# Fetching the residual by pairs of column blocks, and a fourth group of seven products in the down stages' second pair

## The chip, the cores and the metric

The kernel runs on one core of one Trainium2 chip. The metric is the time of one execution on the device, in microseconds (us); lower is better. Before the change it is 1809.0 us, the median of three runs.

## The reference

One layer over 256 rows x of width 2048, all in float32:

```python
x = x + 0.5 * swiglu(rms_norm(x, ffn1_norm), ffn1_w_gate, ffn1_w_up, ffn1_w_down)
h = rms_norm(x, mix_norm);  [u | q | k | v] = h @ w_in
x = x + concat(rms_norm(GLU(S5(u))), rms_norm(stick_breaking(q, k, v))) @ w_out
x = x + 0.5 * swiglu(rms_norm(x, ffn2_norm), ffn2_w_gate, ffn2_w_up, ffn2_w_down)
x = x + rms_norm((p @ w_ple_proj) * sigmoid(rms_norm(x, ple_norm) @ w_ple_gate), ple_post_norm)

def swiglu(h, w_gate, w_up, w_down):
    return (silu(h @ w_gate) * (h @ w_up)) @ w_down      # inner width 5632
```

The change lies in the two products with `w_down`: 256 x 5632 by 5632 x 2048, once in each half FFN.

## The kernel before

**Precision.** A float32 product is made of three matmuls of a rounded type: high by high, low by high and high by low. `split` (L179 to 191) makes both halves of an operand: the high half is an ACT cast (L182), the low half a DVE subtraction (L185) that needs it. A weight is split when it has come in. Its 128x(4x512) float32 tile of 1 MB, called `raw`, comes by one transfer on SP's queue (L369 for a column, L585 for a chunk), into a pool of five raw buffers. Each half of a tile, 128x1024, is one split; its two results go into a ring of seven weight pairs (`weight_pair`, L342: four named `whi`/`wlo`, three `shi`/`slo`). DVE thus cannot be more than seven pairs ahead of TensorE (PE).

**The down stage** (in `ffn`, from L826 to `pools.close()`) has the 5632 inner positions in 11 blocks `kb` of 512, the 2048 output columns in four blocks of 512, taken as two pairs, and the rows in two tiles `t` of 128. For one pair and one inner block there are two ways:

- a *column* (`column`, L688): each of the two column blocks (side 0, side 1) by itself, 24 matmuls a side in `gemm_half` (L386 high weights, L379 low weights). A side takes one raw tile and two splits. The activation block is split once (`act`, giving `hhi`, `hlo`) and kept for the next use; two such are kept at a time.
- a *chunk* (`chunk`, L663): both sides at once, by seven products in place of eight, 42 matmuls (L567, L570, L572) in place of 48. Its two raw tiles give the quarters b11, b21, b12, b22. DVE makes three sums of them (`add`, L578), POOL issues a transfer that adds b22 to b12 in place (L671), and seven splits follow, products 1, 5, 6, 4, 2, 3, 7 in this order. A chunk also needs the activations in summed form (`sum_forms`: four 128x256 row sums on DVE, L524, and a split into `nhi`, `nlo`).

After a pair's last chunk, `opened` (L839) adds the seven products' sums into the residual x: one ACT copy, two DVE additions from PSUM (L843, L848) and six gathers of 128x512 (`gather`, L837). The remaining columns then finish one side after the other; at each side's end (`end`) two gathers and two transposes (`nxt.block`, L220) start that block's way to the next stage.

**The order** is written out by hand in `plans`, one row per pair: ("c", kb) a column on both sides, ("s", kb) a chunk, ("f", kb) a summed form ahead of its chunk, ("a", ...) the columns that end one side after the other, side 1 in the reversed order. Chunks of pair 2 are 2, 1 and 0; columns 10, 9, 3, 4 and then 5, 6, 7, 8. A scheduler orders the instructions of each engine from this.

**The residual** x is fetched at the start of each down stage (`fetch_x`, L826): eight POOL transfers of 128x512 (L151) into two raw tiles, one for each row tile, from the input in the first FFN and from `scr_x` in the second. They are held until the stage's end, so that three raw buffers are left for weights.

**SP's queue** also carries the finished blocks to the next stage: `turn_quarters` (L233) issues 16 small transfers `h<-mid` for each column block, among the weight loads.

The stages are seen in the trace at about 446 to 704 us (first FFN) and 1445 to 1701 us (second).

Of the kernel before, what the change touches and what calls it, by code (L numbers as in the profile page):

```python
# [9 lines left out]
F32 = mybir.dt.float32  # L10
# [6 lines left out]
P = 128  # L17
# [9 lines left out]
NB = 512  # L27
# [6 lines left out]
def layer_kernel(ctx: ExitStack, tc: tile.TileContext, a: dict, shapes: dict, out: bass.AP):  # L34
# [9 lines left out]
    TT = T // P  # L44
    ND = D // NB
# [8 lines left out]
    wp = ctx.enter_context(tc.tile_pool(name="wts", bufs=4))  # L54
# [8 lines left out]
    def uid(s):  # L63
        count[0] += 1
        return f"{s}_{count[0]}"
# [16 lines left out]
    def small(n=8):  # L82
        return smp.tile([P, 8], F32, tag="sm", name=uid("sm"))[:, :n]
# [24 lines left out]
    def put_off(steps, fn, *args):  # L108


        def g():
            for _ in range(steps):
                yield
            fn(*args)

        return start(g())
# [22 lines left out]

    xt = [[], []]  # L140

    def place_x():
        for t in range(TT):
            x = wp.tile([P, ND, NB], F32, tag="raw", name=uid("x"), bufs=5)
            xt[t][:] = [x[:, n, :] for n in range(ND)]

    def fetch_x(rows):
        place_x()
        for n in range(ND):
            for t in range(TT):  # L150
                nc.gpsimd.dma_start(xt[t][n], rows[t * P : (t + 1) * P, n * NB : (n + 1) * NB])  # L151

    scr_x = dramp.tile([T, D], F32, name="scr_x")
# [361 lines left out]
    def sum_forms(pool, u, kind="n"):  # L515

        sums = pool.tile([P, 2, NB], F32, tag="sum", name=uid("rows"), bufs=2)
        s = sums.rearrange("p j n -> p (j n)").rearrange("p (z j x b) -> p z j x b", z=4, j=2, b=32)
        (a11, a21), (a12, a22) = ([u[:, k : k + 2, 4 * t : 4 * t + 4] for t in range(TT)] for k in (0, 2))
        for z, (x, y, op) in enumerate((  # L520
            (a21, a22, ALU.subtract), (s[:, 0], a11, ALU.subtract),
            (a11, a21, ALU.subtract), (a12, s[:, 1], ALU.add),
        )):
            nc.vector.tensor_tensor(out=s[:, z], in0=x, in1=y, op=op)  # L524
        both = halves(kind)
        split(*both, sums.rearrange("p j n -> p (j n)").rearrange("p (z t) -> p z t", z=4))
        return both
# [175 lines left out]
    def ffn(i, xn, nxt, bg=None):  # L703
# [7 lines left out]
        side = ExitStack()  # L711
# [18 lines left out]
        for f in range(NF):  # L730
# [9 lines left out]
            if f >= early or f in alone:  # L740
# [17 lines left out]
                s = Seven(xn, lambda kb: sums[kb], ((wg, f * NB), (wu, f * NB)), sevens, turns)  # L758
# [64 lines left out]
                )  # L823
            put_off(2, turned, hp, f, hh)

        fetch_x(a["x"][0] if bg else scr_x)  # L826

        def rows(k):
            return hT[k // 2][:, k % 2 * 4 : k % 2 * 4 + 4]
# [6 lines left out]
        def gather(x, ps, scale):  # L836
            nc.vector.scalar_tensor_tensor(out=x, in0=ps, scalar=scale, in1=x, op0=ALU.mult, op1=ALU.add)  # L837

        def opened(s, n):  # L839
# [5 lines left out]
            for t in range(TT):  # L845
# [9 lines left out]
                ("c", 10),  # L855
            ),
            (
                ("c", 10), ("c", 9), ("s", 2), ("c", 3), ("s", 1), ("f", 0), ("c", 4), ("s", 0), ("a", (5, 6, 7, 8)),
            ),
        )  # L860
        parts, forms = {}, {}
# [13 lines left out]
        for n in range(0, ND, 2):  # L875

            def end(side):
                m = n + side
                for t, z in enumerate(((2, 4), (3, 8))[side]):
                    gather(xt[t][m], s.bank(z), 0.5)  # L880
                put_off(0 if m == ND - 2 or m == ND - 1 and m < nxt.early else 2, nxt.block, m)

            s = Seven(kept, summed, ((wd, n * NB), (wd, (n + 1) * NB)), sevens, turns)
            plan = plans[n // 2]
            left = sum(kind == "s" for kind, _ in plan)
            for kind, kb in plan:
                final = (kind, kb) == plan[-1]
                if kind == "f":
                    forms[kb] = sum_forms(sevens, rows(kb))
                    continue  # L890
                if kind == "s":
                    left -= 1
                    s.chunk(kb, () if left else shared)
                    if not left:
                        put_off(0, opened, s, n)
                    continue
                for side in range(2):
                    s.column(side, (kb,) if kind == "c" else kb[:: 1 - 2 * side], final)
                    if final:
                        end(side)  # L900
        pools.close()
# [737 lines left out]

    n1, nm, n2, npl = Normed("ffn1_norm", load_turned), Normed("mix_norm"), Normed("ffn2_norm", kinds="hhnn", late=0), Normed("ple_norm", late=0)  # L1640
    ffn(1, n1, nm, s5_prep)

    w_in = a["w_in"]
# [75 lines left out]
    mix.close()  # L1719

    ffn(2, n2, npl)


# [62 lines left out]
    with sums_phase("sums3") as sevens:  # L1786
        forms = {1: sum_forms(sevens, whole_rows(sevens, npl(1)), "h")}
        s = Seven(npl, forms.get, ((wg, 0), (wg, NB)), sevens, sevens)
# [16 lines left out]
    n = ND - 1  # L1805
# [11 lines left out]
    t = 0  # L1817
    sigmoid(gate, t, next(gates))
    ple(n, t, gate, next(projs))
    s = small(1)  # L1820
# [7 lines left out]
    t = 1  # L1828
# [152 lines left out]
```

## Time and profile before

| | |
|---|---|
| time, median of 3 runs | 1809.0 us (1808.81 to 1809.14) |
| the profiled execution's own time | 1810.11 us |
| its span | 1808.3 us |
| PE busy, 8892 matmuls | 1801.0 us |
| DVE busy | 1614.2 us |
| ACT busy | 1081.4 us |
| first down stage, 446 to 704 us: PE / DVE busy | 257.18 / 236.02 us |
| second down stage, 1445 to 1701 us: PE / DVE busy | 256.00 / 235.54 us |

The profile follows one execution. A row of the timeline gives start, duration, engine, line, operation, output and inputs; a bracket at its end tells how long the engine was idle before it, and what ended that. `xN` joins N such instructions in a row.

### The profile page before, as it was taken

How to read it: one execution, taken by the hardware profiler on the slowest of the kernel's cores; microseconds unless marked ns; L12 is line 12 of the kernel's file. 1: busy time of each engine (PE TensorE's matmuls, PEld its weight loads, DVE VectorE, ACT ScalarE, POOL GpSimd, SP SyncE). 2: the span in 40 equal slices, each digit the busy share in tenths (PEclk: the TensorE clock that was granted, in tenths of full speed). 3: DMA queues.
4: the chain of work that ended last, by engine and by line, in shares of the span. 5: the costliest groups of instructions: out<-in, count | busy, mean ns of one | idle time of the engine just before them, and what ended most of it. 6: DMA issues, size and time to landing. Idle time of an engine off the chain costs nothing.

```text
span 1808.3 us, 24274 instructions
## 1 busy us (share of the span) xinstructions
PE 1801.0 (100%) x8892; PEld 1492.8 (83%) x8892; DVE 1614.2 (89%) x1894; ACT 1081.4 (60%) x1264; POOL 137.1 (8%) x196
## 2 busy tenths in 40 slices
PE   9999999999999999999999999999999999999998
PEld 8888888888888878888898888888888888888887
DVE  7998889999999898887867899999999999989875
ACT  7445456555666566456895566555565566666664
POOL 0020100000000001112121000000000000000000
PEclk9999999999999999999999999999999999999999
DMA  9689967787776667765646777776767787666663
GB/s 377 214 277 315 279 220 234 242 268 220 257 248 228 209 237 229 258 244 179 204 153 209 248 278 239 266 263 222 233 232 248 236 273 244 231 209 221 206 245 128
DMA packets 108662, 430.49 MB, mean 238 GB/s; under 512 B 24608, under 2 KB 48576, under 8 KB 66144
## 3 DMA queue, kind: packets, MB, share of 16 engines
q1 hardware_dynamic: 96096, 390.10, 60.9%
q0 software_dynamic: 12160, 38.55, 10.0%
q8 instruction: 69, 1.13, 0.2%
q14 instruction: 49, 0.40, 0.1%
q10 hardware_dynamic: 288, 0.31, 0.1%
HBM read 372.41 MB, written 10.88 MB: 212 GB/s over the span
## 4 chain that ended last, share of the span: by engine, by line
PE 90%; DVE 4%; DMA 2%; issue 1%; SPq 1%; ACT 1%; DVEq 0%; ACTq 0%; POOL 0%; POOLq 0%
PE acc L386 29%; PE acc L379 15%; PE aux L386 13%; PE aux L379 7%; PE acc L567 5%; PE acc L572 5%; PE acc L570 5%; PE aux L570 3%; PE aux L567 3%; PE aux L572 3%; DMA raw<-in_ffn_w_down 2%; DVE wlo L185 1%; SPq L233 1%; DVE slo L185 1%; DVE sum L578 1%
## 5 line engine op out<-in xcount | busy, mean ns | idle before, releaser
L185 DVE TENSOR_TENSOR wlo<-raw,whi 128x1024 fp32r<-128x1024 f32 x478 | 576.3, 1221 | 96.7 <-ACT whi L182 94.6
L182 ACT CAST whi<-raw 128x1024 fp32r<-128x1024 f32 x478 | 495.2, 1050 | 267.2 <-PE acc L386 139.8
L386 PE MATMUL acc<-whi,nhi 128*128 128x512 f32 x850 | 331.7, 392 | 0.0
L386 PE MATMUL acc<-whi,nlo 128*128 128x512 f32 x850 | 329.7, 389 | 0.0
L379 PE MATMUL acc<-wlo,nhi 128*128 128x512 f32 x850 | 240.5, 389 | 0.1
L185 DVE TENSOR_TENSOR slo<-raw,shi 128x1024 fp32r<-128x1024 f32 x186 | 226.2, 1216 | 8.7 <-ACT shi L182 7.2
L182 ACT CAST shi<-raw 128x1024 fp32r<-128x1024 f32 x186 | 195.1, 1049 | 42.1 <-DMA raw<-in_ffn_w_down 22.5
L182 ACT CAST whi<-sum 128x1024 fp32r<-128x1024 f32 x83 | 87.5, 1054 | 168.8 <-DVE sum L578 159.3
L386 PEld LDWEIGHTS acc<-whi,nhi 128*128 128x128 f32 x850 | 159.7, 188 | 33.7 <-ACT whi L182 0.2
L379 PEld LDWEIGHTS acc<-wlo,nhi 128*128 128x128 f32 x850 | 159.4, 188 | 33.7 <-DVE wlo L185 0.5
L386 PEld LDWEIGHTS acc<-whi,nlo 128*128 128x128 f32 x850 | 159.6, 188 | 32.4
L182 ACT CAST shi<-sum 128x1024 fp32r<-128x1024 f32 x61 | 64.3, 1054 | 105.5 <-DVE sum L578 104.8
L671 POOL DMA_DIRECT2D raw<-raw x47 | 41.4, 880 | 1034.8 <-DVE sum L578 827.9
L578 DVE TENSOR_TENSOR sum<-sum,raw 128x1024 f32<-128x1024 f32 x96 | 117.1, 1220 | 0.9
L185 DVE TENSOR_TENSOR wlo<-sum,whi 128x1024 fp32r<-128x1024 f32 x83 | 101.2, 1221 | 3.1 <-ACT whi L182 2.2
L386 PE MATMUL aux<-whi,nhi 128*128 128x512 f32 x244 | 95.0, 389 | 0.0
L386 PE MATMUL aux<-whi,nlo 128*128 128x512 f32 x244 | 94.9, 389 | 0.0
L185 DVE TENSOR_TENSOR slo<-sum,shi 128x1024 fp32r<-128x1024 f32 x61 | 74.5, 1221 | 0.7
L379 PE MATMUL aux<-wlo,nhi 128*128 128x512 f32 x244 | 75.1, 389 | 0.0
L578 DVE TENSOR_TENSOR sum<-raw,raw 128x1024 f32<-128x1024 f32 x48 | 58.5, 1219 | 5.3 <-DMA raw<-in_ffn_w_down 5.2
L567 PE MATMUL acc<-whi,hhi 128*128 128x512 f32 x154 | 60.2, 391 | 0.0
L570 PE MATMUL acc<-whi,hlo 128*128 128x512 f32 x154 | 59.9, 389 | 0.0
(427 smaller groups left out, 3539.7 us busy)
## 6 DMA issues: line engine op xcount, KB each, us to landing
raw<-in_ffn_w_down SPq DMA_DIRECT2D x88, 1024.0 KB, 4.9
raw<-in_ffn_w_gate SPq DMA_DIRECT2D x87, 1024.0 KB, 7.3
raw<-in_ffn_w_up SPq DMA_DIRECT2D x87, 1024.0 KB, 5.6
raw<-in_w_in SPq DMA_DIRECT2D x32, 1024.0 KB, 5.7
raw<-raw POOLq DMA_DIRECT2D x50, 512.0 KB, 5.7
raw<-in_w_out SPq DMA_DIRECT2D x16, 1024.0 KB, 4.9
raw<-in_w_ple_gate SPq DMA_DIRECT2D x16, 1024.0 KB, 5.3
hT<-mid SPq DMA_DIRECT2D x160, 64.0 KB, 4.7
```

Source lines behind the costliest of these rows:

```text
L182: copy = nc.scalar.copy(hi, src)
L185: rest = nc.vector.tensor_tensor(out=lo, in0=src, in1=hi.bitcast(F32), op=ALU.subtract)
L233: nc.sync.dma_start(out[32 * q : 32 * q + 32].rearrange("p (t i w) -> p t i w", t=TT, i=4)[:, :, i], mid[32 * i : 32 * i + 32, q].rearrang ...
L379: nc.tensor.matmul(ps[t], lhsT=lh, rhs=lo[:, j, cols], start=False, stop=stop and j == 1, skip_group_check=joined,)
L386: nc.tensor.matmul(ps[t], lhsT=(ahi, alo)[i][:, 2 * h + j, t * P : (t + 1) * P], rhs=hi[:, j, cols], start=start and j == 0 and i == 0, st ...
L567: nc.tensor.matmul(ps, lhsT=lh[j], rhs=hi[:, j], start=begin and j == 0, stop=False, skip_group_check=joined)
L570: nc.tensor.matmul(ps, lhsT=ll[j], rhs=hi[:, j], start=False, stop=False, skip_group_check=joined)
L572: nc.tensor.matmul(ps, lhsT=lh[j], rhs=lo[:, j], start=False, stop=z in final and j == 1, skip_group_check=joined)
L578: nc.vector.tensor_tensor(out=t, in0=x, in1=y, op=ALU.add)
L671: nc.gpsimd.dma_start(b12, b22, accum_op=ALU.add)
```

## The change

`place_x` goes; `fetch_x` gets a pair as its argument and fetches only that pair's two column blocks, for both row tiles, into one raw tile. Pair 0 is fetched where all of x was before, so that four raw buffers are left for weights; the second pair's fetch is an entry ("x", 1) of the second plan, after chunk 0, from where three are left. In the second plan block 5 becomes a chunk, with its summed form just ahead; blocks 4 and 6 have their side 0 ahead of it, through a new entry ("o", kb), and their side 1 at the end, and the last entry now gives each side's columns itself.

```diff
-    def place_x():
-        for t in range(TT):
-            x = wp.tile([P, ND, NB], F32, tag="raw", name=uid("x"), bufs=5)
-            xt[t][:] = [x[:, n, :] for n in range(ND)]
-
-    def fetch_x(rows):
-        place_x()
-        for n in range(ND):
+    def fetch_x(rows, pair):
+        x = wp.tile([P, ND, NB], F32, tag="raw", name=uid("x"), bufs=5)
+        for n in range(2 * pair, 2 * pair + 2):
             for t in range(TT):
+                xt[t][n] = x[:, 2 * t + n % 2, :]
                 nc.gpsimd.dma_start(xt[t][n], rows[t * P : (t + 1) * P, n * NB : (n + 1) * NB])
...
-        fetch_x(a["x"][0] if bg else scr_x)
+        fetch_x(a["x"][0] if bg else scr_x, 0)
...
-                ("c", 10), ("c", 9), ("s", 2), ("c", 3), ("s", 1), ("f", 0), ("c", 4), ("s", 0), ("a", (5, 6, 7, 8)),
+                ("c", 10), ("c", 9), ("s", 2), ("c", 3), ("s", 1), ("f", 0), ("o", 4), ("s", 0), ("x", 1), ("o", 6),
+                ("f", 5), ("s", 5), ("a", ((7, 8), (8, 7, 6, 4))),
...
+                if kind == "x":
+                    fetch_x(a["x"][0] if bg else scr_x, kb)
+                    continue
...
-                for side in range(2):
-                    s.column(side, (kb,) if kind == "c" else kb[:: 1 - 2 * side], final)
+                for side in range(1 if kind == "o" else 2):
+                    s.column(side, kb[side] if kind == "a" else (kb,), final)
```

What DVE does in the first FFN's second pair after the split for chunk 0's fourth product (`slo` of a `sum`, the first row of each piece). `raw`, `sum`, `rows` and `hT` are weight tiles, their sums, row sums and activations; before, `raw_1077` and `raw_1085` are the first ending columns:

```order
L185 TENSOR_TENSOR slo_1068_5744<-sum_1066_5741,shi_1067_5743 128x1024
L185 TENSOR_TENSOR slo_1072_5764<-raw_1055_5700,shi_1071_5763 128x1024
L185 TENSOR_TENSOR wlo_1074_5774<-raw_1055_5700,whi_1073_5773 128x1024
L185 TENSOR_TENSOR hlo_1076_5784<-hT2_449_2679,hhi_1075_5783 128x1024
L185 TENSOR_TENSOR wlo_1079_5790<-raw_1077_5787,whi_1078_5789 128x1024
L185 TENSOR_TENSOR slo_1081_5794<-raw_1077_5787,shi_1080_5793 128x1024
L837 SCALAR_TENSOR_TENSOR x_757_4236<-sg_1082_5809,x_757_4236 128x512
L837 SCALAR_TENSOR_TENSOR x_757_4236<-acc_988_5350,x_757_4236 128x512
```

and with the change, where `raw_1072` is block 6 and `raw_1080` and `raw_1081` are chunk 5:

```order
L181 TENSOR_TENSOR slo_1062_5705<-sum_1060_5702,shi_1061_5704 128x1024
L181 TENSOR_TENSOR slo_1066_5725<-raw_1049_5661,shi_1065_5724 128x1024
L181 TENSOR_TENSOR wlo_1068_5735<-raw_1049_5661,whi_1067_5734 128x1024
L181 TENSOR_TENSOR hlo_1071_5750<-hT3_581_3325,hhi_1070_5749 128x1024
L181 TENSOR_TENSOR slo_1074_5756<-raw_1072_5753,shi_1073_5755 128x1024
L181 TENSOR_TENSOR wlo_1076_5760<-raw_1072_5753,whi_1075_5759 128x1024
L520 TENSOR_TENSOR rows_1077_5787<-hT2_449_2679 128x256 x2
L520 TENSOR_TENSOR rows_1077_5787<-rows_1077_5787,hT2_449_2679 128x256
L181 TENSOR_TENSOR hlo_1083_5801<-hT2_449_2679,hhi_1082_5800 128x1024
L520 TENSOR_TENSOR rows_1077_5787<-hT2_449_2679,rows_1077_5787 128x256
L574 TENSOR_TENSOR sum_1084_5804<-raw_1080_5796,raw_1081_5798 128x1024
L181 TENSOR_TENSOR wlo_1086_5808<-raw_1080_5796,whi_1085_5807 128x1024
```

Where the gathers into x began, one side of block 6 and the chunk's sums and splits now stand; the gathers come after chunk 5's last split.

SP's queue around chunk 2's two loads (L585 before, L581 with the change) and the load of column 3 (`raw_1004`, `raw_1003`), with the transfers of the first pair's blocks (`h<-mid`) between them. Before:

```order
L369 DMA raw_973_5286<-in_ffn1_w_down 128x2048
L233 DMA h_956_5191<-mid_955_5190 32x2x128 x4
L585 DMA raw_978_5324<-in_ffn1_w_down 128x2048
L233 DMA h_956_5191<-mid_955_5190 32x2x128 x2
L585 DMA raw_979_5326<-in_ffn1_w_down 128x2048
L233 DMA h_956_5191<-mid_955_5190 32x2x128 x6
L233 DMA h_963_5229<-mid_955_5190 32x2x128 x4
L233 DMA h_956_5191<-mid_955_5190 32x2x128 x4
L233 DMA h_963_5229<-mid_955_5190 32x2x128 x8
L369 DMA raw_1004_5440<-in_ffn1_w_down 128x2048
```

With the change:

```order
L365 DMA raw_972_5281<-in_ffn1_w_down 128x2048
L581 DMA raw_977_5319<-in_ffn1_w_down 128x2048
L229 DMA h_955_5186<-mid_954_5185 32x2x128 x4
L581 DMA raw_978_5321<-in_ffn1_w_down 128x2048
L229 DMA h_955_5186<-mid_954_5185 32x2x128 x8
L229 DMA h_962_5224<-mid_954_5185 32x2x128 x4
L229 DMA h_955_5186<-mid_954_5185 32x2x128 x4
L229 DMA h_962_5224<-mid_954_5185 32x2x128 x8
L365 DMA raw_1003_5435<-in_ffn1_w_down 128x2048
```

Chunk 2's first load has moved ahead of all of these transfers, its second two places up; the load of column 3 still has 28 of them ahead of it.

POOL's queue over the second pair, before:

```order
L671 DMA raw_915_4997<-raw_915_4997 128x1024
L671 DMA raw_979_5326<-raw_979_5326 128x1024
L671 DMA raw_1019_5534<-raw_1019_5534 128x1024
L671 DMA raw_1055_5700<-raw_1055_5700 128x1024
L1269 MEMSET m3_1132_6123 128x2048
```

With the change, where `x_1069` is the second part of x and `raw_1049` belongs to chunk 0:

```order
L667 DMA raw_978_5321<-raw_978_5321 128x1024
L667 DMA raw_1018_5529<-raw_1018_5529 128x1024
L147 DMA x_1069_5744<-in_x 128x512 x4
L667 DMA raw_1049_5661<-raw_1049_5661 128x1024
L667 DMA raw_1081_5798<-raw_1081_5798 128x1024
```

The fetch stands ahead of chunk 0's accumulating transfer, though the plan has it after that chunk, and chunk 5's is new.

## The prediction

> **What bounds the kernel now.** I read the page first. Three of its lines say where to look: the span, the busy times, and the chain of work that ended last.
>
> ```profile
> span 1808.3 us, 24274 instructions
> PE 1801.0 (100%) x8892; PEld 1492.8 (83%) x8892; DVE 1614.2 (89%) x1894; ACT 1081.4 (60%) x1264; POOL 137.1 (8%) x196
> PE 90%; DVE 4%; DMA 2%; issue 1%; SPq 1%; ACT 1%; DVEq 0%; ACTq 0%; POOL 0%; POOLq 0%
> ```
>
> PE is idle for 1808.3 - 1801.0 = 7.3 us of the whole span, so nothing that only lets data come sooner can gain more than that. DVE is second with 89%, but that is an average. The view by windows, over the middle of the second pair of either down stage, shows the local share (columns: window, length, busy time of PE, PEld, DVE, ACT, POOL with instructions, clock, DMA share, GB/s):
>
> ```profile
> 612.00:669.00 57.00, 57.00 (x253) 47.22 (x252) 53.05 (x56) 37.53 (x42) 1.77 (x2) 1.00 0.69 240
> 1611.00:1668.00 57.00, 57.00 (x253) 47.22 (x252) 53.97 (x57) 38.45 (x42) 1.73 (x2) 1.00 0.73 244
> ```
>
> PE has no gap, and DVE lacks 57 - 53.05 = 3.95 us. What DVE waits for in these two windows is short:
>
> ```profile
> DVE wlo L185 <- ACT whi L182: 3.1, 1, 3.1
> DVE sum L578 <- DMA raw<-in_ffn_w_down: 0.4, 1, 0.4
> ```
> ```profile
> DVE slo L185 <- ACT shi L182: 3.3, 1, 3.3
> ```
>
> One wait in each window is nearly all of DVE's idle time. After it, DVE works without a pause while PE does too: two engines at their limit, and DVE is never more than a pair or two ahead. The timelines give both paces. PE (column block 3's first matmul, and the same place 12 matmuls on):
>
> ```profile
> 618.08 0.39 PE L386 MATMUL acc<-whi,hhi 128*128 128x512 f32 x1
> 620.80 0.39 PE L386 MATMUL acc<-whi,hhi 128*128 128x512 f32 x1
> ```
>
> So a matmul takes 2.72 / 12 = 0.2267 us. DVE:
>
> ```profile
> 611.17 1.22 DVE L185 TENSOR_TENSOR hlo<-hT,hhi 128x1024 fp32r<-128x1024 f32 x1
> 615.46 2.36 DVE L185 TENSOR_TENSOR wlo<-raw,whi 128x1024 fp32r<-128x1024 f32 x2 [3.07 <-ACT whi L182]
> ...
> 634.69 0.42 DVE L524 TENSOR_TENSOR rows<-rows,hT 128x256 f32<-128x256 f32 x1
> 635.02 0.42 DVE L524 TENSOR_TENSOR rows<-hT 128x256 f32<-128x256 f32 x1
> ...
> 636.83 1.22 DVE L185 TENSOR_TENSOR slo<-raw,shi 128x1024 fp32r<-128x1024 f32 x1
> 637.97 1.22 DVE L185 TENSOR_TENSOR nlo<-rows,nhi 128x1024 fp32r<-128x1024 f32 x1
> 639.10 1.22 DVE L185 TENSOR_TENSOR wlo<-raw,whi 128x1024 fp32r<-128x1024 f32 x1
> ...
> 652.39 1.23 DVE L185 TENSOR_TENSOR slo<-sum,shi 128x1024 fp32r<-128x1024 f32 x1
> ...
> 659.21 0.69 DVE L837 SCALAR_TENSOR_TENSOR x<-sg,x 128x512 f32<-128x512 f32 x1
> 659.82 1.28 DVE L837 SCALAR_TENSOR_TENSOR x<-acc,x 128x512 f32<-128x512 f32 x2
> ```
>
> The starts are (639.10 - 636.83) / 2 = 1.135 us apart for a 128x1024 operation (a split's second half, or an addition; "wide" below), 0.33 for a row sum, 0.61 for a 128x512 gather. I price by starts, since rows of 1.22 us overlap. [...] By full lengths the total below would be about 4 us higher.
>
> **The change part by part.**
>
> *Seven products for block 5 in place of two columns.* A chunk has 42 matmuls, two columns have 48: -6 in each of the two down stages, -12 x 0.2267 = **-2.72 us** of PE. On DVE a chunk needs 10 wide operations (3 sums, 7 splits) = 11.4 us against 42 x 0.2267 = 9.52 of PE: it eats the lead. A column on both sides has 4 splits and an activation split = 5.7 against 10.88: it builds lead. The change trades the second for the first and adds a summed form (4 row sums and a split, 1.3 + 1.1 us).
>
> [...]
>
> *DVE's lead at chunk 0.* Before, its fourth product needs its second half at:
>
> ```profile
> 654.34 0.62 PE L572 MATMUL acc<-slo,hhi 128*128 128x512 f32 x2
> ```
>
> DVE ends that split at 652.39 + 1.23 = 653.62, a lead of 0.72. Afterwards block 4 has one side before chunk 0, so PE asks 24 x 0.2267 = 5.44 earlier, at 648.90; DVE has two splits less, 2.27, and starts earlier. Why earlier: SP's queue before,
>
> ```profile
> 588.84 0.53 SPq L585 DMA_DIRECT2D raw<-in_ffn_w_down  x1
> ...
> 591.99 0.33 SPq L585 DMA_DIRECT2D raw<-in_ffn_w_down  x1
> 592.37 16.03 SPq L233 DMA_DIRECT2D h<-mid  x22
> 608.50 0.53 SPq L369 DMA_DIRECT2D raw<-in_ffn_w_down  x1
> ```
>
> and ACT, whose wait ends when that last load lands:
>
> ```profile
> 614.38 2.00 ACT L182 CAST whi<-raw 128x1024 fp32r<-128x1024 f32 x2 [3.62 <-DMA raw<-in_ffn_w_down]
> ```
>
> The load of column 3 stands behind 28 activation transfers and, before, behind two chunk loads among them; the second is issued 3.15 us after the first, of which its buffer's release accounts for 3.15 - 0.53 - 2 x 0.73 (16.03 / 22) = 1.2. With four weight buffers one chunk load stands ahead of those transfers and the other finds its buffer free: 1.2 + 0.33 of issue = 1.5 us earlier at least. The load's own 614.38 - 608.50 = 5.9 us may come down towards the 4.9 of the page's row (below), and the transfers run less beside loads: 2.5 and more. DVE's restart moves from 615.46 to no later than 614 and no earlier than 611.17 + 1.14 = 612.3, where the work ahead ends (611.4 if that activation split is put behind). I take 612.4, near that end. Then chunk 0's split ends at 653.62 - 3.06 - 2.27 - 0.37 (the DMA wait above) = 647.9: lead 1.0, no stall.
>
> *From chunk 0's fourth product to chunk 5's.* PE: a chunk and one side of block 6, 9.52 + 5.44 = 14.96 us. DVE, counted in the changed order: 16 wide operations and 4 row sums, 16 x 1.135 + 4 x 0.33 = 19.5. It loses 4.55 against a lead of 1.0: **a stall of 3.55**. From there to column 8: PE 48 matmuls = 10.88, DVE 6 wide and 8 of 128x512 (the opening of the sums into x) = 6.8 + 4.9 = 11.7, 0.8 more. Together **4.3 us per down stage** (3.3 with restart at 611.4, 5.9 at 614). Later columns have one side each (5.44 of PE against 3.4 of DVE), so DVE recovers and no more is lost. In the second stage DVE restarts after an idle time of the same length, and its lead at chunk 0's fourth product is smaller:
>
> ```profile
> 1613.86 1.22 DVE L185 TENSOR_TENSOR slo<-raw,shi 128x1024 fp32r<-128x1024 f32 x1 [3.28 <-ACT shi L182]
> ...
> 1651.49 1.22 DVE L185 TENSOR_TENSOR wlo<-raw,whi 128x1024 fp32r<-128x1024 f32 x1
> ```
> ```profile
> 1653.14 0.62 PE L572 MATMUL acc<-wlo,hhi 128*128 128x512 f32 x2
> ```
>
> (1653.14 - 1651.49 - 1.22 = 0.43). I take 4.3 for it too: **+8.6** in all.
>
> *A stall that goes.* The first stage has one now, at column 6:
>
> ```profile
> 669.97 0.49 PE L386 MATMUL acc<-whi,hhi 128*128 128x512 f32 x1
> 671.23 0.50 PE L386 MATMUL acc<-whi,hlo 128*128 128x512 f32 x1 [0.76 <-DVE hlo L185]
> ```
>
> 1.26 - 0.23 = 1.03 us. DVE got there late for want of a load of this order of the plan; that place is gone: **-1.03**.
>
> *The second fetch of x.* Four transfers on POOL's queue, ahead of chunk 0's accumulating transfer. They need the buffer of chunk 1's second tile, free after its last split, two splits ahead of the row sums at 634.69 above, so by about 632 or sooner; the accumulation waits for chunk 0's first sum, 7 wide operations before the split that ends at 647.9, so until about 640. The fetch before:
>
> ```profile
> L151 POOL DMA_DIRECT2D x<-in_x x8: 546/562/729, 446.7 to 455.8; - x8
> ```
>
> At 0.56 us each they are issued by 635: no delay. Gathers need x near 672. Priced at nothing; without that cover the accumulation would be late by the difference, 0 to 2 us. Four fetches fewer at the stage's start, and one more raw buffer there, can gain at most what PE lacks of the span.
>
> *Handover.* The last sides have four columns as before, but the next stage's first loads stand behind 12 to 16 activation transfers in place of ahead of them, and at the end of the second stage PE waits already:
>
> ```profile
> 1716.90 0.50 PE L567 MATMUL acc<-shi,nhi 128*128 128x512 f32 x1 [0.59 <-ACT shi L182]
> ```
>
> From this row I bound the extra wait between 0 and 3 us for both stages (up to five times this row, once or twice), **+1.0**, nearer the bottom, since DVE has 4 x 3.4 = 13.6 us of work for 21.8 us of PE there.
>
> *Sum:* -2.72 - 1.03 + 8.6 + 1.0 = **+5.9 us**. The profiled execution took 1810.11 us; with the change 1816.0. The median of the three runs is 1809.0, 1.1 below it, so **1814.9**. With the bounds of each term: -3.75 + 6.6 + 0 = +2.9 to -3.75 + 11.8 + 3 = +11.1, 1811.9 to 1820.1.
>
> **The rivals.** A. *DVE keeps up.* The earlier loads let DVE enter column 3 with enough lead for three chunks. Then only the matmuls count: -2.72, or -3.75 with the old stall gone, 1805.3 to 1806.3. For it: PE is 100% busy on the page, and the fourth buffer is real. Against it: DVE would have to restart 4.3 us sooner, at 608.1, where it still has work of its own up to 612.3. Below a restart at 608.1 this one decides. Chance 0.10.
>
> B. *Half of it.* Some splits stand later in PE's need than I counted, the handover costs nothing: a stall of about 2 per stage, -3.75 + 4 = 0, 1808 to 1812 with what is uncertain in the lead. Chance 0.18.
>
> C. *Loads come late.* After the second fetch three buffers are left for two chunk tiles and a column; chunk 5's second tile takes the buffer that chunk 0's last split frees, two splits after the 647.9 above, 650.2. With 0.33 of issue and a load's median from the page,
>
> ```profile
> raw<-in_ffn_w_down SPq DMA_DIRECT2D x88, 1024.0 KB, 4.9
> ```
>
> it lands at 655.4; DVE comes to its first sum 6 wide operations and 4 row sums after 647.9, at 656.0. The margin is 0.6. A load as slow as the 5.9 us above, or one that shares the DMA with the four x transfers, eats it and adds 2 to 4 us per stage: the sum becomes +9 to +14, 1818 to 1823. Chance 0.10.
>
> **How the numbers follow.** The forecast has 0.62, own range 1811.9 to 1820.1. From 1808.0 to 1820.0 lie the forecast and B; A and most of C, under 0.2, stay out. A measurement tells about 0.2%, 3.6 us, from no change: 1805.4 to 1812.6. Faster: most of A, 0.08. Same: the rest of A, B, and the forecast's lowest part, 0.22. Slower: 0.70.
>
> **What would show it.** Right: PE waits for DVE's `slo` or `wlo` inside chunk 5 in both stages, about 3.5 us, then a little at column 8; DVE's idle window before column 3 shrinks to about nothing; no wait before. Wrong: no PE wait in chunk 5 (A); PE waits whose releaser is a load or POOL's accumulation (C); DVE restarting column 3 before 609; or handover gaps of several us.

## The result, and the profile after

| | before | after |
|---|---|---|
| median on the same chip, 4 runs each | 1808.9 us (1807.53 to 1809.14) | **1820.62 us** (1818.6 to 1822.21) |
| the profiled execution's own time / span | 1810.11 / 1808.3 us | 1822.21 / 1820.4 us |

The changed kernel is slower: ratio 1.0067 (95% interval 1.0056 to 1.0079), 11.7 us on the medians, where 5.9 was forecast. 1820.62 lies just above the range. Lines of the kernel are 4 lower than before (L181 is the split, L365 a column's load, L581 a chunk's).

The page of after:

```profile
span 1820.4 us, 24277 instructions
PE 1805.0 (99%) x8880; PEld 1490.9 (82%) x8880; DVE 1631.6 (90%) x1916; ACT 1091.6 (60%) x1272; POOL 137.0 (8%) x198
PE 87%; DVE 7%; DMA 2%; SPq 2%; issue 2%; ACT 1%; DVEq 0%; ACTq 0%
```

PE has 12 matmuls fewer and is busy 4 us longer; its idle time went from 7.3 to 1820.4 - 1805.0 = 15.4 us. DVE holds 7% of the chain that ended last in place of 4%. To find where, I set the same matmul of both traces side by side through the program. The distance between the two traces grows at five places, in all by 12.1 us:

| place | growth, us | of what |
|---|---|---|
| up to the first down stage | 0.6 | not explained by one wait |
| first down stage, to 704 | 0.3 | 6 matmuls -1.36, old stalls -1.65 (column 6's -1.24 among them), new stalls +3.34 |
| **719 to 726**, chunk 2 of `w_in`, in the next stage | **4.2** | waits of 1.0 and 1.0, and matmuls at half pace |
| **about 764**, a column of `w_in` | **4.1** | one wait of 2.5, and matmuls at half pace |
| second down stage and what follows it | 2.8 | 6 matmuls -1.36, new stalls +3.67, handover +0.5 |

(Stalls are what PE's starts from 640 and 1640 us to the stage's end exceed 0.2267 us apiece.) So the stages that were rebuilt account for little, and two places that the diff does not touch for 8.3 of the 12.1 us. The windows over the two down stages' second pair, and over the stage behind the first, of before:

```profile
641.00:700.00 59.00, 58.18 (x255) 47.32 (x254) 50.32 (x52) 34.04 (x40) 2.69 (x2) 1.00 0.64 221
1640.00:1700.00 60.00, 60.00 (x266) 49.71 (x265) 51.48 (x53) 34.41 (x40) 0.86 (x1) 1.00 0.66 225
700.00:780.00 80.00, 80.00 (x559) 65.77 (x558) 66.49 (x81) 45.44 (x56) 12.03 (x17) 1.00 0.82 269
```

and of after:

```profile
641.00:700.00 59.00, 57.22 (x247) 45.63 (x246) 54.34 (x57) 34.86 (x39) 4.43 (x7) 1.00 0.60 199
1640.00:1700.00 60.00, 58.17 (x251) 46.07 (x250) 59.96 (x65) 39.68 (x44) 3.99 (x6) 1.00 0.62 207
700.00:780.00 80.00, 75.42 (x464) 60.70 (x464) 64.64 (x79) 40.09 (x52) 8.84 (x14) 0.96 0.77 257
```

In the second row DVE has 59.96 of 60 us: the limit that the prediction named is reached. In the third, PE had no gap before and now lacks 4.58 us, at a granted clock of 0.96. PE's waits in 700 to 780 of after (before has none there):

```profile
PE acc L382 <- ACT whi L178: 2.5, 1, 2.5
PE aux L568 <- DVE wlo L181: 1.0, 1, 1.0
PE aux L563 <- ACT whi L178: 1.0, 1, 1.0
```

Three waits make 4.6 us. The other 3.7 is pace. After's timeline behind the longest:

```profile
767.66 0.80 PE L382 MATMUL acc<-whi,nhi 128*128 128x512 f32 x1 [2.53 <-ACT whi L178]
768.25 0.63 PE L382 MATMUL acc<-whi,nlo 128*128 128x512 f32 x1
768.68 0.63 PE L382 MATMUL acc<-whi,nhi 128*128 128x512 f32 x1
```

Matmuls start 0.43 us apart (768.68 - 768.25) where 0.2267 was the pace in before. The clock of that stretch and of the other place:

```profile
718.00:728.00 10.00, 7.96 (x27) 5.64 (x26) 9.85 (x17) 9.97 (x17) 2.16 (x4) 0.83 0.66 181
763.00:773.00 10.00, 7.47 (x27) 5.75 (x26) 9.91 (x10) 5.04 (x5) 3.38 (x4) 0.83 0.84 323
```

What these waits wait for begins in SP's queue. Before, around the end of the first down stage (`h<-mid` is the last blocks' way to the next stage, L585 the two loads of chunk 2):

```profile
680.75 2.85 SPq L369 DMA_DIRECT2D raw<-in_w_in  x2
685.68 11.42 SPq L233 DMA_DIRECT2D h<-mid  x16
697.20 1.00 SPq L585 DMA_DIRECT2D raw<-in_w_in  x2
...
741.51 1.00 SPq L369 DMA_DIRECT2D raw<-in_w_in  x2
...
751.13 4.95 SPq L1253 DMA_DIRECT2D ua<-ub  x8
```

and after:

```profile
686.30 9.12 SPq L229 DMA_DIRECT2D h<-mid  x12
695.52 0.52 SPq L365 DMA_DIRECT2D raw<-in_w_in  x1
696.09 2.50 SPq L229 DMA_DIRECT2D h<-mid  x4
698.69 0.53 SPq L365 DMA_DIRECT2D raw<-in_w_in  x1
...
699.80 5.16 SPq L581 DMA_DIRECT2D raw<-in_w_in  x2
...
745.84 0.51 SPq L365 DMA_DIRECT2D raw<-in_w_in  x1
...
757.04 4.30 SPq L1253 DMA_DIRECT2D ua<-ub  x7
761.44 1.48 SPq L365 DMA_DIRECT2D raw<-in_w_in  x3
```

The first two loads of `w_in` went out at 680.75 and the one behind it, and now at 695.52 and 698.69, behind 12 and 16 small transfers. Chunk 2's two follow while tables of the next part (`m`, `rot` and others) move too. The time from the issue of chunk 2's loads to their landing, of before and then of after:

```profile
DMA to landing us min/median/max: 4.9/5.9/6.8
```
```profile
DMA to landing us min/median/max: 9.8/11.0/12.1
```

At the second place one load of a pair stays at 745.84 and the other has gone behind the eight `ua<-ub` transfers (one at 755.86, seven from 757.04), to 761.44. Those transfers wait for transposes that stand in DVE's order: the pair from 754.51 ends at 755.84, and the first of the eight goes out at 755.86.

### The profile page after: what moved, and what is told of

Read it like the earlier page. It is cut to its first block, busy times and chain, and to the rows that moved or that the text cites. A ratio compares the mean times of both kernels' runs of the same rounds, so it can differ in the third digit from the quotient of the medians.

```text
span 1820.4 us, 24277 instructions
## 1 busy us (share of the span) xinstructions
PE 1805.0 (99%) x8880; PEld 1490.9 (82%) x8880; DVE 1631.6 (90%) x1916; ACT 1091.6 (60%) x1272; POOL 137.0 (8%) x198
## 4 chain that ended last, share of the span: by engine, by line
PE 87%; DVE 7%; DMA 2%; SPq 2%; issue 2%; ACT 1%; DVEq 0%; ACTq 0%
PE acc L382 28%; PE acc L375 14%; PE aux L382 12%; PE aux L375 6%; PE acc L568 5%; PE acc L563 5%; PE acc L566 5%; PE aux L568 3%; PE aux L563 3%; PE aux L566 3%; DVE wlo L181 2%; SPq L229 1%; DVE slo L181 1%; DVE sum L574 1%; DVE x L833 1%
## 5 line engine op out<-in xcount | busy, mean ns | idle before, releaser
L181 DVE TENSOR_TENSOR wlo<-raw,whi 128x1024 fp32r<-128x1024 f32 x477 | 575.2, 1221 | 98.4 <-ACT whi L178 96.7
L181 DVE TENSOR_TENSOR slo<-raw,shi 128x1024 fp32r<-128x1024 f32 x187 | 227.6, 1217 | 10.3 <-ACT shi L178 10.0
L178 ACT CAST whi<-sum 128x1024 fp32r<-128x1024 f32 x87 | 91.6, 1053 | 165.7 <-DVE sum L574 145.9
L574 DVE TENSOR_TENSOR sum<-sum,raw 128x1024 f32<-128x1024 f32 x100 | 122.0, 1220 | 0.7
L181 DVE TENSOR_TENSOR wlo<-sum,whi 128x1024 fp32r<-128x1024 f32 x87 | 106.1, 1222 | 4.5 <-ACT whi L178 3.6
L181 DVE TENSOR_TENSOR slo<-sum,shi 128x1024 fp32r<-128x1024 f32 x63 | 76.9, 1221 | 1.4 <-ACT shi L178 0.7
```

Of the source, the lines that this page charges most:

```text
L178: copy = nc.scalar.copy(hi, src)
L181: rest = nc.vector.tensor_tensor(out=lo, in0=src, in1=hi.bitcast(F32), op=ALU.subtract)
L574: nc.vector.tensor_tensor(out=t, in0=x, in1=y, op=ALU.add)
```

## The experiments

In each, the time is set against before on the same chip. Theories in the expectations: **O**, the static order on SP's queue has moved loads of the next stage behind small transfers; **C**, chunk 2's loads share the DMA with the tables; **X**, the fetch of x by pairs costs it; and the prediction's own, DVE's lateness in the rebuilt stages. All compute the whole layer.

**The fetch and the plan apart.** `x_only` has the fetch by pairs and, for the rest, the old second plan (the edit is shown against the changed kernel, as for all here but the three `behind` kernels and `turn_pool_before`):

```diff
-                ("c", 10), ("c", 9), ("s", 2), ("c", 3), ("s", 1), ("f", 0), ("o", 4), ("s", 0), ("x", 1), ("o", 6),
-                ("f", 5), ("s", 5), ("a", ((7, 8), (8, 7, 6, 4))),
+                ("c", 10), ("c", 9), ("s", 2), ("c", 3), ("s", 1), ("f", 0), ("c", 4), ("s", 0), ("x", 1),
+                ("a", ((5, 6, 7, 8), (8, 7, 6, 5))),
```

> The changed kernel's fetches of x by pairs, with the second plan of before (blocks 4 and 5 as columns). Three theories for the +11.7 us. O (order of loads): the loss sits in the stage after the first FFN, where the scheduler now puts the first loads of w_in behind 12 and 16 of the activation transfers; this kernel has those loads ahead of them again, so -1.5 to +1.5 us against before. D (DVE's work): the loss is the stalls within the two down stages that the extra chunk makes; no extra chunk, so -1.5 to +1.5 us as well. X (second fetch, fewer raw buffers): the loss comes with the late fetch; +8 to +12 us here.

`plan_only` has the new plan and the old fetch of all x at once, with `place_x` and `fetch_x` as they were before (not shown):

```diff
-        fetch_x(a["x"][0] if bg else scr_x, 0)
+        fetch_x(a["x"][0] if bg else scr_x)
...
-                ("c", 10), ("c", 9), ("s", 2), ("c", 3), ("s", 1), ("f", 0), ("o", 4), ("s", 0), ("x", 1), ("o", 6),
+                ("c", 10), ("c", 9), ("s", 2), ("c", 3), ("s", 1), ("f", 0), ("o", 4), ("s", 0), ("o", 6),
...
```

> The new second plan, with all of x fetched into two raw tiles at the stage's start as before. O: the loads of w_in stand behind the activation transfers as in the changed kernel, so +9 to +13 us. D: at least the changed kernel's stalls, +9 to +14, and more of it inside the down stages, since only three raw buffers are left for weights. X: nothing is fetched late, so -4 to +2 us.

`ffn2_only` has the fetch by pairs everywhere and the new plan in the second FFN alone:

```diff
+            if n and bg:
+                plan = (
+                    ("c", 10), ("c", 9), ("s", 2), ("c", 3), ("s", 1), ("f", 0), ("c", 4), ("s", 0), ("x", 1),
+                ("a", ((5, 6, 7, 8), (8, 7, 6, 5))),
+                )
```

> The new second plan in the second FFN alone; x is fetched by pairs in both. O: the first FFN hands over as before, and the part of the loss that the traces show from 1600 us on, +2 to +4 us, is left. D: one of two alike stages, half of the loss, +5 to +7 us. X: both late fetches are still there, +9 to +12 us.

Measured: x_only 1809.51 against 1807.74, ratio 1.0012 (1.0003 to 1.0021), +1.8; plan_only 1821.28, 1.0073 (1.006 to 1.0085), +13.5; ffn2_only 1811.64, 1.0019 (1.001 to 1.0028), +3.9. The plan is the cause and X falls: the new plan alone has the whole loss, with the same three waits (2.5, 1.0 and 0.9 us) behind the first FFN. The second FFN's plan is worth 3.9 - 1.8 = 2.1, which leaves 11.7 - 3.9 = 7.8 for the first one's. x_only's trace has no stall at column 6 either, nor has any later one of the kernel before with a queue moved. So that stall seems to have belonged to the one profiled execution of before; a second trace of that very kernel was not taken.

**Is it the chunk, or the sides?** `c5_col` keeps the split sides and the fetch, with block 5 a column again:

```diff
-                ("f", 5), ("s", 5), ("a", ((7, 8), (8, 7, 6, 4))),
+                ("c", 5), ("a", ((7, 8), (8, 7, 6, 4))),
```

> The changed kernel with block 5 as a column on both sides in the chunk's place; the split of blocks 4 and 6 into one side early and one late, and the second fetch of x, are kept. If the extra chunk, through DVE's work, is what turns the order of the later loads round: 0 to +2.5 us against before, as with x by pairs alone. If the early and late sides or the fetch do it: +7 to +12 us.

1810.57 against 1808.24, 1.0014 (1.0005 to 1.0024), +2.3, no more than x_only within its interval. SP's queue of c5_col:

```profile
677.25 3.96 SPq L365 DMA_DIRECT2D raw<-in_w_in  x2
684.56 11.10 SPq L229 DMA_DIRECT2D h<-mid  x16
```

It has before's order, both column loads ahead of the small transfers. So it is the chunk that turns it. That it does so through the time at which DVE's work frees raw buffers is argued, not tested by itself. PE waits nowhere from 700 to 780.

**The moved loads alone.** The kernel before, with its first two `w_in` loads held behind the small transfers (`behind`), with the one load of the second place held behind `ua<-ub` (`behind2`), and with all three (`behind_both`):

```diff
+        if behind[0]:
+            behind[0] -= 1
+            with tc.issue_after(turned_last[0]):
+                nc.sync.dma_start(raw[:, :nk, :], quarter(w, k0 // 4, n0))
...
+        if calls[0] == 9:
+            with tc.issue_after(u_last[0]):
+                nc.sync.dma_start(raw[:, :nk, :], quarter(w, k0 // 4, n0))
```

> The kernel before, unchanged but for its first two loads of w_in, which are held on SP's queue until 12 and 16 of the activation transfers of column block 2 are issued, as they stand with the change. O: this alone brings back most of what the first handover lost in the trace, +4 to +9 us (4.9 at the first chunk of w_in, and 4 more if the later loads are moved along). D and X: the matmuls and DVE's work and x are those of before, -1 to +1 us.

> The kernel before, with one load of w_in (the ninth column's) held behind the eight transfers of the second block of u, as it stands with the change. Holding the first two loads behind the activation transfers cost only 1 to 2 us, so what is asked is whether this place in the queue by itself makes the wait at 764 us. Q (place in the queue): those transfers wait for DVE's transposes, the load is issued some 12 us late whatever else happens, +3 to +5 us (a wait of 2.7 and matmuls at half pace after it). G (general lateness): without the late work of the stage ahead the load still comes in time, -1 to +2 us.

> The kernel before with all three loads of w_in held where the change has them (behind 12 and 16 activation transfers, and behind the second block of u). If the order of the queue is the whole of the loss after the first FFN: +8 to +10 us. If the first place only costs when DVE and the buffers are late as well: the sum of the two single runs, +5 to +7 us.

behind: 1809.68 against 1807.74, 1.0011 (1.0002 to 1.0021), +1.9, under what O asked for, and PE has no wait there. O as the cause of the first place is not enough. But the loads of w_in's chunk land 4.7 to 7.0 us after their issue there, as the tables go out behind them, so this kernel has the order of the queue and not the collision. behind2: 1812.07 against 1807.63, 1.0025 (1.0014 to 1.0035), +4.4. Its waits from 700 to 780, its PE, and the window of that place:

```profile
PE acc L393 <- ACT whi L182: 2.4, 1, 2.4
```
```profile
760.84 0.50 PE L393 MATMUL acc<-whi,nhi 128*128 128x512 f32 x1 [2.44 <-ACT whi L182]
```
```profile
757.00:767.00 10.00, 7.55 (x27) 5.75 (x26) 9.91 (x11) 5.04 (x5) 3.38 (x4) 0.83 0.87 350
```

Nearly the same wait and the same clock as at after's second place, in a kernel without the change: that place is shown, 4.4 against 4.1. behind_both: 1813.42 (1810.74 to 1816.54) against 1807.5, 1.0031 (1.0018 to 1.0043), +5.9, about the sum of the two. Its spread of 5.8 us is wide; in its longest run, the profiled one, PE waits 1.3 and 0.8 us at the first place too, beside the 2.6 of the second. So with the loads late the first place can be lost in the old kernel too; the spread suggests that it is not lost each time.

**The small transfers out of the way.** `turn_pool` is the changed kernel with the 16 `h<-mid` transfers of the stage's last blocks on POOL's queue; `turn_pool_before` is the kernel before with the same move:

```diff
-    def turn_quarters(out, mid, steps):
+    def turn_quarters(out, mid, steps, queue=nc.sync):
...
-                    nc.sync.dma_start(
+                    queue.dma_start(
...
-                turn_quarters(out, mid, 4 if soon else 6)
+                turn_quarters(out, mid, 4 if soon else 6, nc.gpsimd if soon and self.gain == "mix_norm" else nc.sync)
```

> The changed kernel, with the 16 activation transfers of column block 2 of the first FFN on POOL's queue in place of SP's. The loads of w_in then have none of them ahead, and the scheduler again puts six column loads ahead of the second block of u. Q (place in the queue): both losses after the first FFN go, +2 to +5 us is left (the stalls inside the two down stages and the second hand-over, less 2.7 of matmuls). G: the loads still wait for buffers that a late DVE frees, +9 to +13 us.

> The kernel before, with those 16 activation transfers on POOL's queue: what the move costs or gains by itself. Nothing waits there before, so -1 to +1 us; if POOL's slower issue delays what reads them, +1 to +3 us.

turn_pool: 1814.71 against 1807.63, 1.0039 (1.0024 to 1.0054), +7.1. turn_pool_before: 1809.26 against 1808.24, 1.0004 (0.9995 to 1.0014), no difference. The move is free in the old kernel and takes away 11.7 - 7.1 = 4.6 us of the changed one's loss. It also put the second place's load back, whose wait is gone. Of turn_pool's waits from 700 to 780, the first place's are left:

```profile
PE acc L568 <- DVE wlo L181: 0.9, 1, 0.9
PE acc L563 <- ACT whi L178: 0.5, 1, 0.5
```

**The tables behind the chunk's loads.** `tables_late` is the changed kernel with `m1`, `rot` and `cp` behind chunk 2's second load, on SP. Three transfers of `m3` on POOL still ran beside them, so it did only part of what it should. `m3_late` (the diff) puts those behind the chunk's accumulating transfer, and `turn_m3` is m3_late with turn_pool's move:

```diff
-                nc.sync.dma_start(raw, quarter(w, kb, n0))
+                chunk_load[0] = nc.sync.dma_start(raw, quarter(w, kb, n0)).ins
...
-            nc.gpsimd.dma_start(b12, b22, accum_op=ALU.add)
+            chunk_load[1] = nc.gpsimd.dma_start(b12, b22, accum_op=ALU.add).ins
...
-                nc.sync.dma_start(ld[q][n], scr[n][q])
+                if q:
+                    nc.sync.dma_start(ld[q][n], scr[n][q])
+                else:
+                    with tc.issue_after(chunk_load[0]):
+                        nc.sync.dma_start(ld[q][n], scr[n][q])
...
-                nc.gpsimd.dma_start(m3[p0 : p0 + HC, :, HC * z :], scr_h[g, :, :, : (SL - z) * HC])
+                with tc.issue_after(chunk_load[1]):
+                    nc.gpsimd.dma_start(m3[p0 : p0 + HC, :, HC * z :], scr_h[g, :, :, : (SL - z) * HC])
```

> The changed kernel, with the transfers of the first S5 tables (m1, rot, cp on SP, m3 on POOL) held until the second load of w_in's chunk is issued. C (collision): those 1 MB loads took 10 to 12 us in the trace in place of 4.9 because the tables were moved beside them; without that they land about 5 us sooner and the loss at 719 to 726 us (4.9 us) goes for the most part: +7 to +9 us against before. G (the loads are issued late in any case, for want of free buffers): +11 to +13 us, as the changed kernel.

> The changed kernel, with the first S5 tables held behind the loads of w_in's chunk, this time for certain: m1, rot and cp behind its second load on SP's queue, and all of m3 behind its accumulating transfer on POOL's own queue (in the earlier try three m3 transfers still ran beside the first of these loads, which took 11.6 us). C (collision makes the loads late): the loss at 719 to 726 us shrinks from 4.9 to under 1.5, +7 to +9 us against before. G (they are issued too late for want of buffers): that loss stays over 3 us, +10 to +13 us.

> The same, and the 16 activation transfers of column block 2 on POOL's queue. Loads neither queued behind small transfers nor collided with: if what POOL's queue alone left at 719 to 722 us (1.7 us of waits) was from the tables, nothing of the first hand-over is lost, +4 to +6 us against before (the stalls in the two down stages 2.3 and 2.5, the second hand-over 1.2, less 2.7 for the matmuls, and 1 to 2 for x by pairs). If DVE's own backlog did it, +6.5 to +8 us as with POOL's queue alone.

tables_late: 1818.12 against 1807.63, 1.0059 (1.0044 to 1.0074), +10.5. m3_late: 1818.49 against 1807.5, 1.0058 (1.0043 to 1.0073), +11.0. turn_m3: 1814.37 against 1807.5, 1.0038 (1.0023 to 1.0053), +6.9. In m3_late's trace the loads are back at before's time:

```profile
DMA to landing us min/median/max: 4.9/6.0/7.1
```

and the first place grows by 1.7 us in place of 4.2, with one wait of 1.1 for DVE left; the second place still has its 2.5, and 0.4 behind it.

So C holds for the place, in the trace. The time does not follow fully: against before on its chip the gain is 11.7 - 11.0, less than both intervals can tell. Part of the reason may be that 1.7 of after's 4.2 is a stretch of half pace ((1 - 0.83) x 10 us), and that such stretches come and go between the profiled executions (last section): m3_late's has one inside chunk 5 of the first down stage (a clock of 0.83 over 661 to 671), where after has none (1.00). turn_m3 gains nothing over turn_pool: with the second place and the loads repaired, waits of 0.9 and 0.3 us remain. DVE in the window ahead of them, of before and then of turn_m3:

```profile
704.00:722.00 18.00, 18.00 (x85) 14.97 (x85) 17.62 (x30) 13.08 (x20) 4.36 (x9) 1.00 0.80 226
704.00:722.00 18.00, 17.34 (x80) 13.80 (x78) 17.45 (x30) 12.59 (x20) 2.62 (x4) 1.00 0.69 187
```

DVE is no busier there than in the kernel before, where PE does not wait. That the rest is DVE's backlog from the stage ahead fits, but is not shown.

**Less for DVE.** `c6` puts both sides of block 6 ahead of chunk 5, so that PE has more work there; one column less is left at the end of side 1, and the small transfers begin two steps sooner:

```diff
-                turn_quarters(out, mid, 4 if soon else 6)
-                put_off(9 if soon else 11, self.parted, n, by_tile(out, 4))
+                turn_quarters(out, mid, 2 if soon else 6)
+                put_off(7 if soon else 11, self.parted, n, by_tile(out, 4))
...
-                ("c", 10), ("c", 9), ("s", 2), ("c", 3), ("s", 1), ("f", 0), ("o", 4), ("s", 0), ("x", 1), ("o", 6),
-                ("f", 5), ("s", 5), ("a", ((7, 8), (8, 7, 6, 4))),
+                ("c", 10), ("c", 9), ("s", 2), ("c", 3), ("s", 1), ("f", 0), ("o", 4), ("s", 0), ("x", 1), ("c", 6),
+                ("f", 5), ("s", 5), ("a", ((7, 8), (8, 7, 4))),
```

> The changed kernel with block 6 as a column on both sides ahead of chunk 5 (and one column less at the end of side 1; the activation transfers of block 2 begin two steps sooner, since a later step reads them). DVE gains 2.2 us of lead ahead of chunk 5. D (DVE's lead): the stalls in chunk 5, 2.6 and 2.8 us, go nearly whole, and the later loads come sooner, -3 to +4 us against before. Q (place in the queue): the stalls go, but the loads of w_in and the u transfers stand as in the changed kernel, +5 to +8 us.

1820.84 against 1807.63, 1.0074 (1.0059 to 1.0089), +13.2. The stalls inside chunk 5 shrink to 0.5 (first stage) and 0.6 us, and in the first stage a wait at a column takes their place. c6's waits from 640 to 700 and then, of its rows from 700 to 780, the longest:

```profile
PE acc L375 <- DVE wlo L181: 1.1, 1, 1.1
...
PE acc L382 <- ACT whi L178: 2.7, 1, 2.7
PE aux L563 <- ACT whi L178: 1.0, 1, 1.0
```

The work that DVE lacks time for is the same: the waits behind the stages are no less, 4.9 and 2.6 us where after has 4.6 and 1.0.

`add_pool` gives chunk 5's three sums to POOL, and `add_turn_pool` adds turn_pool's move:

```diff
+            self.adder = nc.vector
...
-            nc.vector.tensor_tensor(out=t, in0=x, in1=y, op=ALU.add)
+            self.adder.tensor_tensor(out=t, in0=x, in1=y, op=ALU.add)
...
+                    s.adder = nc.gpsimd if n and kb in (5,) else nc.vector
```

> The changed kernel with chunk 5's three sums on POOL in place of DVE, 3.4 us less for DVE in each down stage. On SP's queue the ninth column load of w_in then stands ahead of the second block of u again; the first two loads stay behind the activation transfers. By the count of stalls in the traces: the stalls in chunk 5 mostly gone (-3 to -5 us), the wait at 764 us gone (-4.1), the loss at 719 to 726 us kept, so +3 to +6 us against before. Rival: POOL's sums take 3 us and more each (its copies of 128x512 took 1 to 1.9 us), chunk 5 waits for them instead, +6 to +10 us.

> Both: chunk 5's sums on POOL, and the 16 activation transfers of column block 2 after the first FFN on POOL's queue. By the count: 0 to +3 us against before; the gain of 2.7 us for the matmuls shows only if all that is left is the second hand-over. Rival (POOL's sums are slow, or DVE's lateness stays): +5 to +9 us.

add_pool: 1822.59 against 1808.24, 1.0081 (1.0064 to 1.0098), +14.4. add_turn_pool: 1822.15, 1.0077 (1.0062 to 1.0092), +13.9. The two losses behind the first stage are gone in add_pool, where DVE has 3 x 1.135 = 3.4 us less to do. On SP only the load of the second place is back where it was; the first two still stand behind 12 and 16 small transfers, and the chunk's loads land 9.1 to 9.5 us after their issue, yet PE waits nowhere. That fits DVE's lateness as the cause, but does not prove it, for PE itself comes out of the stage 5 us later and asks later for everything. The sums are now what PE waits for, 4.8 and 4.5 us in the two stages, and the granted clock over the span is 0.996 to 0.998 in add_pool's four runs, where before's on that chip have 0.999 and 1.0. POOL in the first, and a DVE split beside it, both of add_pool:

```profile
657.32 4.15 POOL L575 TENSOR_TENSOR sum<-raw,raw 128x1024 f32<-128x1024 f32 x1 [15.29 <-DMA raw<-in_ffn_w_down]
662.65 5.82 POOL L575 TENSOR_TENSOR sum<-sum,raw 128x1024 f32<-128x1024 f32 x2
...
659.21 3.35 DVE L181 TENSOR_TENSOR nlo<-rows,nhi 128x1024 fp32r<-128x1024 f32 x1
```

No version with the chunk in both stages came under +6.9, and none of the fifteen beat the kernel before.

## Why the prediction was wrong

**The direction and its reason were right.** A fourth chunk gives DVE more work than it saves PE, and DVE lost the lead. DVE's own ledger came out to the digit: from chunk 0's fourth product to chunk 5's,

```profile
647.97 1.22 DVE L181 TENSOR_TENSOR slo<-sum,shi 128x1024 fp32r<-128x1024 f32 x1
...
667.48 1.22 DVE L181 TENSOR_TENSOR slo<-sum,shi 128x1024 fp32r<-128x1024 f32 x1
```

667.48 - 647.97 = 19.51 us, and 19.5 was counted. DVE had no wait that the view of waits lists from 640 to 690, nor from 1640 to 1690, so no load was late inside the stage: the prediction's rival C is out. Neither did DVE keep up (A).

**The in-stage stall, 4.3 each, was mis-sized.** It measured 3.3 and 3.7, so 7.0 in all and not 8.6. The wait at column 8 was right: 0.7 in both stages, and 0.8 was counted. Chunk 5 of the first stage lost 2.6, where 3.55 was counted. The second stage lost 1.6 there, and 1.2 at chunk 0 already, where the prediction had no stall though it had read the smaller lead:

```profile
1658.16 0.74 PE L568 MATMUL acc<-wlo,hhi 128*128 128x512 f32 x2 [0.61 <-DVE wlo L181]
```

After's PE around chunk 5 of the first stage:

```profile
649.55 0.61 PE L568 MATMUL acc<-slo,hhi 128*128 128x512 f32 x2
...
664.15 0.50 PE L563 MATMUL aux<-whi,nhi 128*128 128x512 f32 x1 [1.48 <-ACT whi L178]
```

The first is where chunk 0's fourth product takes its second half: DVE ends that at 647.97 + 1.22 = 649.19, a lead of 0.36 where 1.0 was taken (DVE came to column 3 at 612.98 and not at 612.4, and lost the rest on the way). I let PE ask for chunk 5's fourth product 14.96 us later, by the order of the products in the code. The scheduler had put product 2, whose operand needs no sum, ahead of it, and interleaved second halves. In the trace 75 matmuls lie between the two needs and not 66, so that the second came 9 x 0.2267 = 2.0 us later than assumed; the long wait stands at product 6 (664.15).

**The stall that goes, -1.03, was no gain.** It was in the shown execution of before and in no later trace of a kernel with its plan. Medians of before, 1807.5 to 1808.9, lie 1.2 to 2.6 us under that execution's 1810.11. A stall of one profiled run was taken off a median. By luck this error and the 1.6 too much for the stalls partly cancel.

**The step that failed is the handover**, "+1.0, nearer the bottom, since DVE has 4 x 3.4 = 13.6 us of work for 21.8 us of PE there". Behind the first FFN it cost 8.3 in the profiled execution, and some 5.9 by the medians (below); 0 to 3 was allowed for both stages. "Handover gaps of several us" stood among the signs of being wrong, but no rival and no chance went with it. The bound came from a PE wait of 0.59 at the end of the *second* stage, and asked whether DVE recovers in the last sides. It does, in busy time: 25.13 of the 32 us from 672 to 704, where before has 24.12. What does not recover is the order. It was fixed when the program was built, and the scheduler puts three loads of `w_in` elsewhere, as I take it because raw buffers come free later when DVE is later. I had read that the first two stand behind 12 to 16 transfers, and priced it at nearly nothing. The third, behind `ua<-ub`, stands 60 us past the stage, where I had not compared the orders.

What the runs show of each place: the second (4.1) is the one load, alone worth 4.4 (behind2), gone when the order is mended (turn_pool). The first (4.2) needs more than one thing: the chunk's loads at 9.8 to 12.1 us beside the tables are worth 2.5 of it in the trace (m3_late), most of that a stretch of half pace (1.7); the rest, 1.7, comes with a wait for DVE, and why DVE is late there is not shown. The loads behind the small transfers cost +1.9 in the old kernel, without a wait at this place, so how much of the 4.2 is theirs alone is not settled; the old kernel with late loads and the collision as well was not run. Both places are clear when the chunk is a column again (c5_col).

**The sum again**, between the two profiled executions: -2.72 for the matmuls, -1.65 for before's own stalls, +7.0 in the stages, +8.3 behind the first, +0.5 behind the second and +0.6 ahead of the first make +12.0, and the spans differ by 12.1. These two executions lie 1.6 and 1.2 us above their medians, so the trace's share for each place is not the median's. By the runs, 7.8 is left for the first FFN's plan; with 3.3 - 1.36 = 1.9 in its stage, an estimate of 5.9 is left for the handover, still outside the 0 to 3. turn_pool's trace fits its time: -2.72 + 6.6 in the stages + 2.5 at the first place + 0.1 behind the second = 6.5, and 7.1 was measured. x_only's +1.8 for the fetch, which I had priced at nothing, is seen as a wait in no trace, and plan_only, which does without the fetch by pairs, is no faster than the changed kernel. What the fetch costs beside the new plan stays open, as does m3_late's total. The accounts of both stages close with the matmuls counted at 0.2267 us, though no run took them out by themselves.

## What to carry to other kernels

Where orders are fixed at build time, compare every queue past the end of the changed stage before pricing the change: here one load behind eight small transfers, 60 us past the stage, cost 4.4 us by itself (behind2), more than the stall inside either stage (3.3 and 3.7). Price such a load by the reader's need against its new issue time plus a landing time beside what now moves with it (9.8 to 12.1 us here, where before had 4.9 to 6.8), not by whether the busy engine recovers on average. Check a stall that a change is to remove, and a stretch of half pace that it seems to bring, in more than one execution before setting it against a median.

## What was not expected of the hardware

**Matmuls ran at half pace behind some PE waits, and not behind others of the same length.** Behind waits of 2.53 (after) and 2.44 us (behind2) matmuls start 0.43 us apart for a while in place of 0.2267, at 0.83 of the clock over 10 us (0.50 from 768 to 770 in after); (1 - 0.83) x 10 = 1.7 us of loss beside the wait. Behind two waits of 1.01 and 1.03 us, 2.2 us apart, the clock over 718 to 728 was 0.83 as well:

```profile
720.84 0.50 PE L563 MATMUL aux<-whi,hhi 128*128 128x512 f32 x1 [1.01 <-ACT whi L178]
...
723.07 1.22 PE L568 MATMUL aux<-wlo,hhi 128*128 128x512 f32 x2 [1.03 <-DVE wlo L181]
```

But the same waits at the same places did not always have it behind them. m3_late has after's wait of 1.48 in chunk 5 and its wait of about 2.5 at the second place:

```profile
665.15 0.50 PE L565 MATMUL aux<-whi,nhi 128*128 128x512 f32 x1 [1.48 <-ACT whi L178]
...
766.46 0.50 PE L382 MATMUL acc<-whi,nhi 128*128 128x512 f32 x1 [2.52 <-ACT whi L178]
```

The clock over the first of these places, of after and then of m3_late, and over the second of m3_late (after's is above, 0.83):

```profile
661.00:671.00 10.00, 8.38 (x35) 5.85 (x34) 10.00 (x10) 8.26 (x9) 0.00 (x0) 1.00 0.44 114
661.00:671.00 10.00, 8.42 (x29) 6.04 (x29) 10.00 (x10) 7.95 (x9) 0.03 (x1) 0.83 0.42 88
762.00:772.00 10.00, 7.08 (x30) 5.22 (x29) 9.91 (x10) 5.04 (x5) 3.39 (x4) 1.00 0.82 320
```

So the wait of 1.48 us has half pace behind it in m3_late and not in after, and the one of 2.5 us in after and not in m3_late. What decides over these 1.7 us is not shown here.

**An addition on POOL cost 2.9 to 4.2 us, and some of DVE's work beside it was slower.** In add_pool 128x1024 took 4.15 and 5.82 / 2 = 2.91 us on POOL against 1.22 on DVE. Of the DVE splits beside these additions, the one at 659.21 took 3.35 and one at 667.13 took 2.43 in place of 1.22; the one at 658.01 took 1.21. By these rows an addition over 1024, beside DVE's own work, took 2.4 to 3.4 times as long on POOL.
